# Hybrid transformer trunk on one core: the overflow loop three groups earlier, squares in the last group, second mixer's norm on VectorE

## The chip, the core and the metric

The kernel runs on one core of one Trainium2 chip. The metric is the device time of one execution in microseconds (us). A core has TensorE (PE; PEld are its weight loads), VectorE (DVE), ScalarE (ACT) and GpSimd (POOL), which work on tiles of 128 partitions in on-chip memory; matrix products are summed in eight PSUM banks. SyncE (SP) issues nearly all DMA transfers, in the order of its queue.

## What is computed

Two layers run over 256 latent and 256 context tokens of width 1024, in float32. Each layer is a mixer and a mixture of experts, each behind an RMS norm with shift and scale and added to the residual stream `h`. Layer 0's mixer is attention beside a gated delta net, layer 1's an RWKV-7. Cut to what matters:

```python
def rms_norm(x, gain):
    xf = x.astype(jnp.float32)
    y = xf * lax.rsqrt(jnp.mean(xf * xf, -1, keepdims=True) + EPS)
    return (y * gain.astype(jnp.float32)).astype(x.dtype)

def centred_shift(x):
    xp = jnp.pad(x, ((0, 0), (1, 1), (0, 0)))
    return 0.5 * (xp[:, :-2] + xp[:, 2:]) - x

# rwkv7_project: xx = centred_shift(x); xr, xw, xk, xv, xa, xg = [x + xx * mu[i] for i in range(6)]

# hier_moe: each token goes to 2 of the 32 experts of one layer; for a block of tokens xb of expert e
        hid = jax.nn.silu(xb @ w1[e]) * (xb @ w3[e])
        return out.at[toks].add((hid @ w2[e]) * ws[:, None]), None
```

An expert's `w1`, `w3` and `w2` are 2 MB each. All 32 experts of both layers are read in every execution.

## The kernel before

`h` is held as eight channel blocks of 128 x 512 (channels x tokens). `Trunk.run` calls the first mixer, `moe` for layer 0, the second mixer and `moe` for layer 1. A scheduler of the programming layer places the instructions of straight-line code on each engine's queue; it doesn't move them across a loop.

**The mixture.** `moe` serves the 32 experts in groups that share the 128 rows of a tile: two experts with up to 64 tokens each (a pair) or four with up to 32 (a quad). Layer 0 has 13 groups, here numbered 0 to 12: 8 and 12 are quads, 9 to 11 pairs. Layer 1 has 8 quads. Layer 0 orders its experts by load at run time (`sort`), so the loads of expert weights take their address from a register that SP reads from the table `order`. One group (`group`) does this: gather the group's tokens by one-hot products with the split tokens `ft` (two halves, each transposed), multiply by `w1` and `w3`, form the gated hidden rows, transpose them, multiply by `w2`, split the result in a high and a low part, and spread it back over the tokens with one product per channel block; `stt` on VectorE adds each to `h[k]` in two halves. `pipe(gens, 2)` keeps two groups in work, so that one group's gather stands between another's products. In the last group (`last`) the products with `w2` go expert by expert.

**Weights.** `weight` loads 1 MB at a time (`s<-in_moe_w` in the trace, line 173) into slots of the pool `big`, which has 21; `h` takes 2 of them and layer 0's `ft` 4. SP waits for a free slot and for the load eight before. Each group also takes one slot for its result `y`.

**Overflow jobs.** Tokens above an expert's share are left for jobs of up to 128 tokens. Their number `num` is only known at run time, so they are the body of a hardware loop, `tc.For_i(0, jobs, 1)` (line 794). All engines read the count and meet at the loop's start and end. With the inputs given no job is left, in either layer, and the body isn't run. `cut` says how many groups come ahead of the loop: all 13 in layer 0, 6 of 8 in layer 1. Where groups are left behind it, the loads of the next group's first weights (up to five) are issued ahead of it (`ahead`). `then` is `mixer1_weights`, which loads the second mixer's first weights.

**The norm.** `norm` squares the eight blocks on ACT (`squares`), adds them up in two sums on VectorE and GpSimd, sums over partitions with a product by ones, and takes logarithm and exponential for the inverse root. Each block is then multiplied (GpSimd in the second mixer) and scaled and shifted in two halves on ACT. The first mixer's norm, called with `between`, multiplies mostly on VectorE and then waits for the modulation. In the second mixer `each` follows per block: `xs` is the sum of the neighbours (VectorE or GpSimd), with its edges copied on GpSimd; two `stt` on VectorE give the shift `xx` and the operand `xk`, from which four matrix products per block start the keys.

Of the kernel before, what the change touches and what calls it, by code (L numbers as in the profile page):

```python
# [12 lines left out]
AF = mybir.ActivationFunctionType  # L13
OP = mybir.AluOpType
# [3 lines left out]
NTOK = 512  # L18
# [100 lines left out]
class Trunk:  # L119
# [169 lines left out]
                self.nc.vector.tensor_copy(h[k], ps)  # L289
        return h  # L290

    def squares(self, h, n):

        sums = [None, None]
        for k in range(8):
            sq = self.tmp()
            self.act(sq[:, :n], h[k], AF.Square)
            if k < 2:
                sums[k] = sq
            else:  # L300
                s = sums[k % 2]
                self.tt(s[:, :n], s[:, :n], sq[:, :n], OP.add, self.nc.vector if k % 2 else self.nc.gpsimd)
        return sums

    def norm(self, h, l, which, between=None, each=None):

        n = NTOK

        self.act(self.small([1, 1], "lnt"), self.eps[0:1, 5:6], AF.Ln)
        sums = self.squares(h, n)  # L310
        ps = self.bank()
        for i in range(2):
            self.mm(ps[:, :n], self.c["ones"], sums[i][:, :n], start=i == 0, stop=i == 1)
        rs = self.tmp()
        self.act(rs[:, :n], ps[:, :n], AF.Ln, bias=self.eps[:, 0:1], scale=1.0 / D)
        self.act(rs[:, :n], rs[:, :n], AF.Exp, scale=-0.5)
        u = self.chan(n)
        if between:
            for k in range(8):
                self.tt(u[k], h[k], rs, OP.mult, self.nc.gpsimd if k % 3 == 2 else None)  # L320
            between()
        for k in range(8):
            if not between:
                self.tt(u[k], h[k], rs, OP.mult, self.nc.gpsimd)
            for s in range(2):
                a = self.amul[:, l, which, k, s:s + 1]
                b = self.mcol[l][:, 3 * which, k, s:s + 1]
                x = u[k][:, 256 * s:256 * s + 256]
                if s and between:
                    self.ts(x, x, a, b, OP.mult, OP.add)  # L330
                else:
                    self.act(x, x, AF.Identity, scale=a, bias=b)
            if each:
                each(k, u[k])
        return u
# [299 lines left out]
        self.mm(out, r(onehot), r(hi), start, False)  # L635
        self.mm(out, r(onehot), r(lo), False, stop)

    def moe(self, l, h, lo, ahead, tokens, then=None):
        nc, c, I, tc = self.nc, self.c, self.I, self.tc
        n = NTOK - lo  # L640
        nt = n // 128
        logits, split = tokens
        sid, w, cnt, last, chosen = self.router(logits, nt)
# [4 lines left out]
        if l == 0:  # L648
            pairs = [((p, p + 1), (64, 64)) for p in range(5, 19, 2)]
            quads = [((p, p + 1, p + 2, p + 3), (32,) * 4) for p in range(19, 31, 4)]  # L650
            specs = [((0, 1), (64, 64)), ((2, 3), (64, 64)), ((4, 31), (96, 32)), pairs[0], quads[0]] + pairs[1:4]
# [2 lines left out]
            specs = [((p, p + 1, p + 2, p + 3), (32,) * 4) for p in range(0, 32, 4)]  # L654
        fixed = 4 if l == 0 else 32

        cut = (len(specs), 6)[l]
        table = order = sp = wp = None
        t4 = lambda: self.tmp(nt * 128).rearrange("p (t s) -> p t s", t=nt)
        half = lambda i: slice(512 * i, 512 * i + 512)  # L660
# [1 line left out]
        def group(P, wt, load, caps, last=False):  # L662
# [65 lines left out]
            for k in range(8):  # L728
                ps = self.bank()

                r = lambda a: a.bitcast(F32R)
                self.mm(ps[:, :n], r(y[:, 0, k, :]), r(PT), True, False)
                self.mm(ps[:, :n], r(y[:, 1, k, :]), r(PT), False, True)
                for s in range(lo // 256, 2):
                    ss = slice(256 * s - lo, 256 * s - lo + 256)
                    self.stt(h[k][:, ss], ps[:, ss], self.mcol[l][:, 5, k, s:s + 1], h[k][:, ss], OP.mult, OP.add)
                if k == 3:
                    yield

        def experts(spec, last):  # L740
            cols, caps = spec
            P = t4()
            step = cols[1] - cols[0]
            cs = slice(cols[0], cols[-1] + 1, step)
            places, weights = (sid, w) if cols[0] < fixed else (sp, wp)
            if len(set(caps)) == 1:
                G, cap = len(caps), caps[0]
                self.tt(P.rearrange("p t (g s) -> p t g s", g=G).bitcast(F32R),
                        c["iota"][:, None, None, :cap].to_broadcast([128, nt, G, cap]),
                        places[:, :, cs][:, :, :, None].to_broadcast([128, nt, G, cap]), OP.is_equal)  # L750
            else:
                a = 0
                for p, cap in zip(cols, caps):
                    self.tt(P[:, :, a:a + cap].bitcast(F32R), c["iota"][:, None, :cap].to_broadcast([128, nt, cap]),
                            places[:, :, p:p + 1].to_broadcast([128, nt, cap]), OP.is_equal)
                    a += cap
            yield
            regs = {}

            def load(name, g):  # L760
                p = cols[g]
                if p < fixed:
                    return ahead.pop((name, p), None) or self.weight(I[name][l, p])
                if p not in regs:
                    regs[p] = nc.sync.value_load(order[0:1, p:p + 1], min_val=0, max_val=31)
                return self.weight(I[name][l, bass.ds(regs[p], 1)].rearrange("o a b -> (o a) b"))

            yield from group(P, weights[:, :, cs], load, caps, last)

        def extra():  # L770
# [11 lines left out]
            sp, wp, order, rank = self.sort(nt, sid, cnt, chosen)  # L782
        table, num = self.overflow(nt, cnt, rank)
        drain(pipe(gens[:cut], 2))
        if cut >= len(specs):
            if then:
                then()
                then = None
        else:
            e0 = specs[cut][0][0]  # L790
            for name, g in [(m, g) for m in ("moe_w1", "moe_w3") for g in range(4)][:5]:
                ahead[name, e0 + g] = self.weight(I[name][l, e0 + g])
        jobs = nc.values_load(num, min_val=0, max_val=40, skip_runtime_bounds_check_because="counts bound it")
        with tc.For_i(0, jobs, 1):  # L794
            drain(extra())
# [638 lines left out]
    def mixer1(self, h):  # L1434
# [20 lines left out]
        def each(k, uk):  # L1455
            us = uk.rearrange("p (s t) -> p s t", s=2)
            xs = xx[k].rearrange("p (s t) -> p s t", s=2)
            self.tt(xs[:, :, 1:255], us[:, :, 0:254], us[:, :, 2:256], OP.add, nc.gpsimd if k % 2 else None)
            nc.gpsimd.tensor_copy(xs[:, :, 0:256:255], us[:, :, 1:255:253])
            self.stt(xx[k], xx[k], 0.5, uk, OP.mult, OP.subtract)  # L1460
            self.stt(xk[k], xx[k], mu[:, 2, k:k + 1], uk, OP.mult, OP.add)
            for m in range(4):
                self.mm(pk[m], wk0[k][:, 128 * m:128 * m + 128], xk[k], k == 0, k == 7)

        u = self.norm(h, 1, 0, each=each)
        pw, pa = self.bank(), self.bank()
        for i, w, ps in ((1, w1, pw), (4, a1, pa)):
            x = self.chan()
# [581 lines left out]
    def run(self):  # L2050
        h, u, fill = self.begin()
        ahead, tokens = self.mixer0(h, u, fill)
        self.mixer1_ahead()
        self.moe(0, h, 0, ahead, tokens, self.mixer1_weights)
        hl, ahead, tokens = self.mixer1(h)
        self.moe(1, hl, 256, ahead, tokens)
        self.store(hl)
# [26 lines left out]
```

## Time and profile before

| | |
|---|---|
| time, median of 3 runs | 2285.43 us |
| lowest of the 3 | 2277.39 us |
| profiled execution, its own time | 2273.31 us |
| its span, first to last instruction | 2271.5 us |
| TensorE busy, share of the span | 1899.7 us, 84% |
| VectorE, ScalarE, GpSimd busy | 834.1, 579.7, 367.0 us |
| mean granted TensorE clock | 0.885 of full |
| moved by DMA | 574.71 MB |

The trace is of one execution. A row of the timeline gives start, duration, engine, line, operation, output and input by the program's names, and the count of instructions merged in it; in brackets stands the idle time ahead of it and what ended that. A matrix product in float32 shows as two entries. Layer 0's mixture lies at about 615 to 1100 us, the second mixer to about 1780, layer 1's mixture to about 2265.

### The profile page before, as it was taken

What the parts mean: (1) busy time and instruction counts of PE and PEld (TensorE: products, weight loads), DVE (VectorE), ACT (ScalarE), POOL (GpSimd) and SP (SyncE); (2) the same over time, 40 slices, a digit from 0 to 9 for tenths busy, and PEclk for the clock granted to TensorE, in tenths of its full rate; (3) what the DMA queues carried; (4) which work ended last, traced back from release to release, by engine and by line L of the source; (5) the groups of instructions that cost most, each with busy time, mean ns of one, the idle gap of its engine ahead of it and who ended that gap; (6) DMA issues with size and microseconds to landing.
All of it is one profiled execution on the core that took longest, in us unless ns stands there. A gap on an engine that the chain in (4) does not pass through costs nothing.

```text
span 2271.5 us, 32246 instructions
## 1 busy us (share of the span) xinstructions
PE 1899.7 (84%) x12738; PEld 1066.3 (47%) x12738; DVE 834.1 (37%) x1885; ACT 579.7 (26%) x1200; POOL 367.0 (16%) x606
## 2 busy tenths in 40 slices
PE   5996899899899888998599599889897876666577
PEld 2443576567443344443245467757786522222222
DVE  3357335542432223132544955563823311111101
ACT  3363223330111111111324524534423100000000
POOL 1034154310000000000503731432501000000000
PEclk7998899999799999999799787787889788788789
DMA  9631132760099999999253543371865399999995
GB/s 312 221 130 38 43 113 100 264 249 22 1 387 421 421 421 421 421 421 417 90 186 101 171 151 140 113 258 59 302 209 221 138 422 421 422 421 421 386 422 247
DMA packets 161227, 574.71 MB, mean 253 GB/s; under 512 B 26218, under 2 KB 61073, under 8 KB 108593
## 3 DMA queue, kind: packets, MB, share of 16 engines
q1 hardware_dynamic: 158704, 572.36, 65.1%
q8 instruction: 102, 1.67, 0.3%
q10 hardware_dynamic: 2369, 0.25, 0.1%
q14 instruction: 52, 0.43, 0.1%
HBM read 537.66 MB, written 34.90 MB: 252 GB/s over the span
## 4 chain that ended last, share of the span: by engine, by line
PE 22%; DMA 18%; DVE 6%; issue 2%; ACT 2%; POOL 2%; SPq 0%; ACTq 0%; DVEq 0%; POOLq 0%
PE b L202 21%; DMA s<-in_moe_w 17%; DVE s L184 2%; DVE kb L184 1%; DVE s L193 1%; ACT t L197 1%; POOL s L184 1%; ACT s L197 1%; DVE t L184 1%; POOL t L184 1%; PE b L206 0%; DMA s<-vD 0%; DMA s<-kD 0%; DVE s L1940 0%; DVE t L1725 0%
## 5 line engine op out<-in xcount | busy, mean ns | idle before, releaser
L202 PE MATMUL b<-s 64*64 64x64 f32 (+7 forms) x5840 | 727.1, 300 | 59.0 <-DVE s L193 30.8
L202 PEld LDWEIGHTS b<-s 128*64 128x64 f32 (+4 forms) x5840 | 489.2, 163 | 294.7 <-issue 167.8
L202 PE MATMUL b<-s,kb 128*32 128x512 f32 (+1 forms) x2112 | 367.3, 654 | 81.1 <-DMA s<-in_moe_w 81.1
L202 PE MATMUL b<-s,t 128*32 128x512 f32 (+4 forms) x1544 | 349.6, 563 | 50.8 <-DMA s<-in_moe_w 24.9
L197 ACT ACTIVATE t<-b 128x512 f32<-128x512 f32 (+3 forms) x161 | 91.8, 573 | 729.8 <-PE b L202 446.3
L202 PEld LDWEIGHTS b<-s,t 128*32 128x32 f32 (+2 forms) x1544 | 156.4, 147 | 209.2 <-issue 125.9
L202 PEld LDWEIGHTS b<-s,kb 128*32 128x32 f32 (+1 forms) x2112 | 97.6, 126 | 327.2 <-issue 209.6
L197 ACT ACTIVATE s<-b 64x256 f32<-64x256 f32 (+6 forms) x228 | 114.4, 505 | 434.4 <-PE b L202 393.8
L202 PE MATMUL b<-t,s 128*128 128x512 f32 (+3 forms) x592 | 156.9, 411 | 16.7 <-ACT s L197 8.9
L184 DVE TENSOR_TENSOR s<-b,s 128x512 fp32r<-128x512 f32 (+3 forms) x90 | 52.8, 606 | 272.1 <-ACT s L197 264.5
L193 DVE SCALAR_TENSOR_TENSOR s<-b,mcol,s 128x256 f32<-128x256 f32 x296 | 120.9, 478 | 80.4 <-PE b L202 80.2
L206 PE MATMUL b<-cst,t 128*128 128x128 f32 (+1 forms) x466 | 79.5, 301 | 75.3 <-DVE t L193 35.3
L202 PEld LDWEIGHTS b<-t,s 128*128 128x128 f32 (+2 forms) x592 | 97.4, 197 | 74.9 <-ACT s L197 26.3
L206 PEld LDWEIGHTS b<-cst,t 128*128 128x128 f32 (+1 forms) x466 | 56.9, 161 | 121.6 <-issue 43.3
L193 DVE SCALAR_TENSOR_TENSOR t<-t,wc,b 128x512 f32<-128x512 f32 x21 | 15.7, 747 | 201.0 <-PE b L202 201.0
L1448 POOL MEMSET s<- 64x1024 f32 x2 | 1.9, 946 | 533.1 <-DVEq L794 533.1
L193 DVE SCALAR_TENSOR_TENSOR t<-t,b 128x512 f32<-128x512 f32 x21 | 14.5, 689 | 172.6 <-ACT t L197 172.6
L197 ACT ACTIVATE kb<-b 128x512 f32<-128x512 f32 (+2 forms) x92 | 50.1, 546 | 105.9 <-PE b L202 72.5
L202 PE MATMUL b<-t,cst 128*128 128x512 f32 (+6 forms) x64 | 36.6, 689 | 40.4 <-POOL t L184 19.3
L206 PE MATMUL b<-cst,s 128*128 128x128 f32 (+1 forms) x332 | 55.5, 303 | 17.3 <-DMA s<-in_ctx 8.2
L202 PE MATMUL b<-s,cs 128*32 128x512 f32 x384 | 53.8, 653 | 6.9 <-DMA s<-in_ada_w 6.3
L184 POOL TENSOR_TENSOR kb<-s 128x23 f32<-128x23 f32 (+11 forms) x115 | 46.4, 404 | 74.8 <-DVE s L1059 67.0
(241 smaller groups left out, 1676.6 us busy)
## 6 DMA issues: line engine op xcount, KB each, us to landing
s<-in_moe_w SPq DMA_DIRECT2D x384, 1024.0 KB, 19.8
s<-in_ada_w SPq DMA_DIRECT2D x48, 1024.0 KB, 8.7
s<-in_hy_w_in SPq DMA_DIRECT2D x8, 1024.0 KB, 5.0
sD<-s SPq DMA_DIRECT2D x8, 1024.0 KB, 4.5
s<-zD SPq DMA_DIRECT2D x8, 1024.0 KB, 5.5
s<-sD SPq DMA_DIRECT2D x8, 1024.0 KB, 8.1
s<-in_hy_w_out SPq DMA_DIRECT2D x4, 1024.0 KB
s<-in_rk_wk SPq DMA_DIRECT2D x4, 1024.0 KB, 9.0
```

The lines of the kernel that those rows point to most:

```text
L184: (eng or self.nc.vector).tensor_tensor(out=out, in0=a, in1=b, op=op)
L193: self.nc.vector.scalar_tensor_tensor(out, a, s, b, op0=op0, op1=op1)
L197: self.nc.scalar.activation(out, a, func, bias=bias, scale=scale)
L202: self.nc.tensor.matmul(out, lhsT, rhs, start=start, stop=stop, skip_group_check=skip)
L206: self.nc.tensor.transpose(out, a, self.c["ident"][:n, :n])
L1448: nc.gpsimd.memset(twa[64 * d:64 * d + 64].rearrange("p (i d t) -> p i d t", i=2, d=2)[:, :, 1 - d], 0.0)
```

## The change

`cut` is 10 in layer 0: the loop stands between groups 9 and 10, and the loads of group 10's `w1` and `w3` are issued ahead of it through `fetch`; registers are read again behind it. `then` is called after the last group. That group calls `tail(k)` after each updated block: `squares` now squares one block, adds it to its neighbour's on VectorE and sums each pair over partitions, so the product by ones is made four times. `norm` takes those sums as `ps`. In the second mixer the multiplication, the neighbour sums (VectorE) and the edge copies (ACT) leave GpSimd.

```diff
-    def squares(self, h, n):
...
+    def squares(self, ps, sums, h, k):
+
+        sq = self.tmp()[:, :NTOK]
+        self.act(sq, h[k], AF.Square)
+        sums.append(sq)
+        if k % 2:
+            self.tt(sums[k - 1], sums[k - 1], sq, OP.add)
+            self.mm(ps, self.c["ones"], sums[k - 1], k == 1, k == 7)
+
+    def norm(self, h, l, which, between=None, each=None, ps=None):
...
-        sums = self.squares(h, n)
-        ps = self.bank()
-        for i in range(2):
-            self.mm(ps[:, :n], self.c["ones"], sums[i][:, :n], start=i == 0, stop=i == 1)
+        if ps is None:
+            ps, sums = self.bank(), []
+            for k in range(8):
+                self.squares(ps, sums, h, k)
...
             if not between:
-                self.tt(u[k], h[k], rs, OP.mult, self.nc.gpsimd)
+                self.tt(u[k], h[k], rs, OP.mult)
...
-        cut = (len(specs), 6)[l]
+        cut = (10, 6)[l]
...
+                if last and tail:
+                    tail(k)
                 if k == 3:
                     yield
+
+        regs = {}
+
+        def fetch(name, p):
+            if p < fixed:
+                return self.weight(I[name][l, p])
+            if p not in regs:
+                regs[p] = nc.sync.value_load(order[0:1, p:p + 1], min_val=0, max_val=31)
+            return self.weight(I[name][l, bass.ds(regs[p], 1)].rearrange("o a b -> (o a) b"))
...
         drain(pipe(gens[:cut], 2))
-        if cut >= len(specs):
-            if then:
-                then()
-                then = None
-        else:
-            e0 = specs[cut][0][0]
-            for name, g in [(m, g) for m in ("moe_w1", "moe_w3") for g in range(4)][:5]:
-                ahead[name, e0 + g] = self.weight(I[name][l, e0 + g])
+        cols = specs[cut][0]
+        for name, p in [(m, p) for m in ("moe_w1", "moe_w3") for p in cols][:5]:
+            ahead[name, p] = fetch(name, p)
+        regs.clear()
         jobs = nc.values_load(num, min_val=0, max_val=40, skip_runtime_bounds_check_because="counts bound it")
...
-            self.tt(xs[:, :, 1:255], us[:, :, 0:254], us[:, :, 2:256], OP.add, nc.gpsimd if k % 2 else None)
-            nc.gpsimd.tensor_copy(xs[:, :, 0:256:255], us[:, :, 1:255:253])
+            self.tt(xs[:, :, 1:255], us[:, :, 0:254], us[:, :, 2:256], OP.add)
+            self.act(xs[:, :, 0:256:255], us[:, :, 1:255:253])
...
-        u = self.norm(h, 1, 0, each=each)
+        u = self.norm(h, 1, 0, each=each, ps=self.sums)
...
+        self.sums, sq = None, []
+
+        def tail(k):
+            if k == 0:
+                self.sums = self.bank()
+            self.squares(self.sums, sq, h, k)
+
-        self.moe(0, h, 0, ahead, tokens, self.mixer1_weights)
+        self.moe(0, h, 0, ahead, tokens, self.mixer1_weights, tail)
```

What this does to TensorE's queue in layer 0 is seen behind group 9's products with `w2`. `t` is the one-hot tile or hidden rows, `s` a slot (weights, tokens or `y`), `kb` the gathered tokens, `cst` the identity, `o_w` the weights of the tokens; in a gather the product reads `s,t` at 128x512, in the products with `w1` and `w3` it reads `s,kb` at 64x512, with `w2` `s,t` at 64x512, and in the output `t,s`. Before, from group 9's output to group 10's products with `w2`:

```order
L202 MATMUL b<-t,s 128x512 x4
L202 MATMUL b<-s,t 128x512 x8
L202 MATMUL b<-t,s 128x512 x4
L206 MATMUL b<-cst,t 128x128 x4
L202 MATMUL b<-s,t 128x512 x8
L206 MATMUL b<-cst,t 128x128 x8
L202 MATMUL b<-o_w,t 128x2 x4
L202 MATMUL b<-t,s 128x512 x8
L202 MATMUL b<-s,kb_5923 64x512 x32
```

After, from the loop's end on (the loop's body is left out), to group 11's output:

```order
L788 UNCONDITIONAL_BRANCH
L202 MATMUL b<-s,t 128x512 x8
L206 MATMUL b<-cst,t 128x128 x4
L202 MATMUL b<-s,t 128x512 x8
L206 MATMUL b<-cst,t 128x128 x8
L202 MATMUL b<-o_w,t 128x2 x4
L202 MATMUL b<-s,kb_6173 64x512 x16
```

```order
L202 MATMUL b<-s,kb_6173 64x512 x16
L202 MATMUL b<-s,kb_6245 64x512 x16
L206 MATMUL b<-cst,t 128x128 x4
L202 MATMUL b<-s,kb_6245 64x512 x16
L202 MATMUL b<-s,t 64x512 x10
L206 MATMUL b<-cst,t 128x128 x4
L202 MATMUL b<-s,t 64x512 x6
L202 MATMUL b<-t,s 128x512 x8
L202 MATMUL b<-s,t 64x512 x2
L202 MATMUL b<-t,s 128x512 x8
L202 MATMUL b<-s,t 64x512 x14
L202 MATMUL b<-t,s 128x512 x16
```

Group 9's output of 16 now stands whole ahead of the loop, and group 10's gather starts behind it; between the two blocks shown stands group 11's gather, of the same five rows. Groups 10 and 11 then run side by side, and group 12's gather follows group 11's output.

On VectorE, at the end of layer 0, `s<-b,mcol` are the updates of `h`, `t<-t` the sums of squares, `s<-s,t` the norm's product, `s<-s 128x2x254` the neighbour sums. Before, from the last updates through the loop (its body left out) to the second mixer's first operand:

```order
L184 TENSOR_TENSOR s<-b,s 128x8x64 x2
L193 SCALAR_TENSOR_TENSOR s<-b,mcol_97,s 128x256 x16
L793 TENSOR_LOAD j_num
L794 COMPARE_AND_BRANCH
...
L569 MEMSET j_tab 128x32
L582 MEMSET j_tab 128x32
L184 TENSOR_TENSOR t<-t 128x512 x3
L184 TENSOR_TENSOR s<-s 128x2x254 x2
L193 SCALAR_TENSOR_TENSOR s<-s 128x512
L193 SCALAR_TENSOR_TENSOR s<-s,mu 128x512
```

After, over the same work:

```order
L184 TENSOR_TENSOR s<-b,s 128x8x64 x2
L193 SCALAR_TENSOR_TENSOR s<-b,mcol_97,s 128x256 x4
L184 TENSOR_TENSOR t<-t 128x512
L193 SCALAR_TENSOR_TENSOR s<-b,mcol_97,s 128x256 x6
L184 TENSOR_TENSOR t<-t 128x512
L193 SCALAR_TENSOR_TENSOR s<-b,mcol_97,s 128x256 x6
L184 TENSOR_TENSOR t<-t 128x512 x2
L184 TENSOR_TENSOR s<-s,t 128x512 x4
L184 TENSOR_TENSOR s<-s 128x2x254 x4
L193 SCALAR_TENSOR_TENSOR s<-s 128x512 x4
L193 SCALAR_TENSOR_TENSOR s<-s,mu 128x512
```

The loop is gone from this place, the sums of squares stand between the updates, and norm and shift go in fours of blocks on VectorE alone.

## Rows read from the trace of the kernel before

**Rows 1.** The page: span, and the expert loads (count, size, us to landing).

```profile
span 2271.5 us, 32246 instructions
...
s<-in_moe_w SPq DMA_DIRECT2D x384, 1024.0 KB, 19.8
```

**Rows 2.** Windows: start:end, length, busy us (count) of each engine, clock, DMA share, GB/s.

```profile
core 0: us, PE busy (x) PEld busy (x) DVE busy (x) ACT busy (x) POOL busy (x), PEclk, DMA share, GB/s
905.00:1047.00 142.00, 126.82 (x633) 62.02 (x631) 37.17 (x86) 20.61 (x36) 0.00 (x0) 0.98 1.01 421
```

**Rows 3.** Waits of TensorE, 905 to 1095: us in total, times, longest.

```profile
PE b L202 <- DMA s<-in_moe_w: 6.6, 3, 3.8
```

**Rows 4.** Timeline of TensorE, groups 9 to 12 of layer 0.

```profile
948.81 7.08 PE L202 MATMUL b<-s,kb 128*64 128x512 f32 x30 [0.55 <-DMA s<-in_moe_w]
...
966.51 1.20 PE L202 MATMUL b<-t,s 128*128 128x512 f32 x4 [0.69 <-ACT s L197]
...
992.70 2.11 PE L202 MATMUL b<-s,t 128*128 128x512 f32 x8
...
1000.58 7.14 PE L202 MATMUL b<-s,t 128*64 128x512 f32 x32
...
1048.04 7.92 PE L202 MATMUL b<-s,kb 128*32 128x512 f32 x70
...
1058.29 7.05 PE L202 MATMUL b<-s,kb 128*32 128x512 f32 x58 [2.32 <-DMA s<-in_moe_w]
...
1067.68 22.59 PE L202 MATMUL b<-s,t 128*32 128x512 f32 x64 [0.69 <-ACT t L197]
```

**Rows 5.** Windows around the loop of layer 1.

```profile
2144.00:2148.00 4.00, 0.00 (x0) 0.00 (x0) 0.00 (x0) 0.00 (x0) 0.00 (x0) 0.50 0.54 225
2148.00:2152.00 4.00, 2.04 (x4) 1.17 (x4) 0.76 (x2) 0.00 (x0) 0.00 (x0) 0.50 0.45 119
2152.00:2160.00 8.00, 6.62 (x23) 4.20 (x22) 0.62 (x4) 2.67 (x5) 0.00 (x0) 0.50 1.02 426
```

**Rows 6.** Timeline behind the loop of layer 1.

```profile
2149.48 0.76 DVE L184 TENSOR_TENSOR t<-cst,r_sid 128x256 fp32r<-128x256 f32 x2 [16.07 <-DMA s<-in_moe_w]
2149.96 2.08 PE L202 MATMUL b<-s,t 128*128 128x512 f32 x4 [18.88 <-DVE t L184]
2158.35 1.92 PE L202 MATMUL b<-s,kb 128*32 128x512 f32 x4
```

**Rows 7.** Timeline from layer 0's last output into the second mixer.

```profile
1090.96 4.00 PE L202 MATMUL b<-t,s 128*128 128x512 f32 x16 [0.69 <-ACT s L197]
1093.13 6.36 DVE L193 SCALAR_TENSOR_TENSOR s<-b,mcol,s 128x256 f32<-128x256 f32 x16 [1.50 <-PE b L202]
1099.87 4.28 ACT L197 ACTIVATE t<-s 128x512 f32<-128x512 f32 x8 [8.96 <-DVEq L794]
...
1106.59 3.78 PE L202 MATMUL b<-t,cst 128*128 128x512 f32 x4 [11.63 <-POOL t L184]
...
1110.41 0.69 ACT L197 ACTIVATE t<-b,eps 128x512 f32<-128x512 f32 x1 [4.96 <-PE b L202]
...
1112.41 0.63 ACT L197 ACTIVATE t<-t 128x512 f32<-128x512 f32 x1
...
1122.27 5.62 PE L202 MATMUL b<-s 128*128 128x512 f32 x8 [11.90 <-DVE s L193]
...
1125.05 1.10 ACT L197 ACTIVATE s<-s,mcol,amul 128x256 f32<-128x256 f32 x2 [0.58 <-POOL s L184]
...
1126.08 1.75 DVE L193 SCALAR_TENSOR_TENSOR s<-s 128x512 f32<-128x512 f32 x1
...
1129.56 22.58 PE L202 MATMUL b<-s 128*128 128x512 f32 x52 [1.67 <-DVE s L193]
...
1143.12 0.68 DVE L193 SCALAR_TENSOR_TENSOR s<-s 128x512 f32<-128x512 f32 x1
```

**Rows 8.** Loads of weights, 2090 to 2200: shortest, median, longest way to landing.

```profile
DMA to landing us min/median/max: 5.3/19.8/20.1
```

More of the change, by code (lines that the diff above doesn't have):

```diff
@@ L290, in load_h @@
         return h
-    def squares(self, h, n):
[L294 to L299, printed above, removed]
-            else:
[L301 to L305, printed above, removed]
+    def squares(self, ps, sums, h, k):
[6 more added lines that the diff above has]
+    def norm(self, h, l, which, between=None, each=None, ps=None):
         n = NTOK
         self.act(self.small([1, 1], "lnt"), self.eps[0:1, 5:6], AF.Ln)
-        sums = self.squares(h, n)
-        ps = self.bank()
-        for i in range(2):
-            self.mm(ps[:, :n], self.c["ones"], sums[i][:, :n], start=i == 0, stop=i == 1)
+        if ps is None:
+            ps, sums = self.bank(), []
+            for k in range(8):
+                self.squares(ps, sums, h, k)
         rs = self.tmp()
@@ L636, in pick, with moe @@
         self.mm(out, r(onehot), r(lo), False, stop)
-    def moe(self, l, h, lo, ahead, tokens, then=None):
+    def moe(self, l, h, lo, ahead, tokens, then=None, tail=None):
         nc, c, I, tc = self.nc, self.c, self.I, self.tc
@@ L757, in experts @@
             yield
[L758 to L766, printed above, removed]
+            load = lambda name, g: ahead.pop((name, cols[g]), None) or fetch(name, cols[g])
             yield from group(P, weights[:, :, cs], load, caps, last)
@@ L784, in moe @@
         drain(pipe(gens[:cut], 2))
-        if cut >= len(specs):
-            if then:
-                then()
-                then = None
-        else:
-            e0 = specs[cut][0][0]
-            for name, g in [(m, g) for m in ("moe_w1", "moe_w3") for g in range(4)][:5]:
-                ahead[name, e0 + g] = self.weight(I[name][l, e0 + g])
+        cols = specs[cut][0]
+        for name, p in [(m, p) for m in ("moe_w1", "moe_w3") for p in cols][:5]:
+            ahead[name, p] = fetch(name, p)
+        regs.clear()
         jobs = nc.values_load(num, min_val=0, max_val=40, skip_runtime_bounds_check_because="counts bound it")
```

## The prediction, made before the changed kernel was run

> **What bounds the kernel now.** I read the page first, then the weight stream's stretch, then both loops, then the gap between layer 0's mixture and layer 1's mixer. The profiled span is 2271.5 us; expert weights arrive as 384 loads of 1 MB [rows 1]. Between 905 and 1047 us, in the later half of layer 0's mixture, DMA moves 421 GB/s, so one load takes 1.0486 MB / 421 GB/s = 2.49 us, and TensorE is busy for 126.8 of 142 us [rows 2]. So two resources stand near their limit, and the question is which has room. From 905 to 1095 us TensorE waited for weights only 6.6 us in all, three times [rows 3]. The last two of them are in the timeline: 0.55 us at 948.8 and 2.32 us at 1058.3 [rows 4]. Between those two, TensorE took every weight later than it landed: there it, and not DMA, sets the pace, with 2.3 us to spare at the end of the stretch. A hole cut into TensorE there comes out at the end except for 2.3 us.
>
> The loop in layer 1 shows what an overflow loop in mid-stream does, with no jobs to run (nothing of its body executes). TensorE's idle time before it was 18.88 us, and VectorE's 16.07 us ended on a weight load: the loop starts only when every load issued ahead of it has landed [rows 6]. DMA falls to 225 and 119 GB/s for two stretches of 4 us, against 421: (1 - 344/842) x 8 = 4.7 us of stream lost. The granted clock is 0.50 there and still 0.50 to 2160 us [rows 5].
>
> **The loop in layer 0 moved to after group 9.** I count groups 0 to 12. When does the drain end? At 948.8 the third load of group 9's w3 landed; until the last of group 10's w3 come 1 + 4 (w2) + 4 + 4 = 13 loads, x 2.49 = 32.4, so 981.2. SP's order up to there is that of before. In layer 1 the stream's equivalent end is 2144 + 4 x 225/421 = 2146.1 and TensorE restarts at 2149.96, 3.8 later [rows 5, 6]; VectorE's comparison ahead of it is twice as wide in layer 0, +0.3. Restart: 985.3. Without a next group to interleave, TensorE ends group 9's output at 966.5 + 4.0 = 970.5 [rows 4, 7], and VectorE's 6.4 us behind it are over by 977: both wait for DMA. TensorE stands 14.8 us.
>
> The gather that follows takes 1000.58 - 992.70 = 7.9 us at full clock [rows 4]. In layer 1 after the loop it took 2158.35 - 2149.96 = 8.4 at half clock, and there it has 4 matmuls where layer 0 has 8, twice, 2.08 per 4 [rows 6]: 8.4 + 4.2 = 12.6. So w1 of group 10 starts at 997.9. From there to w1 of group 12 TensorE does, in the order shown, six passes of 7.14 over a pair's weights, two gathers of 7.9, two outputs of 4.0 with 0.7 of waiting ahead of each [rows 4, 7]: 42.8 + 15.8 + 9.4 = 68.0, so 1065.9. Before it was 1048.0: 17.9 late. The 2.3 us wait for w3 disappears, as those weights land earlier than TensorE now asks. Group 12's w2 starts 15.6 us late, and its 22.6 us and all behind are unchanged. **+15.6.**
>
> Is DMA covered? Of 21 slots h holds 2 and the split tokens 4; group 10's prefetch holds 8, so 7 loads go out at once, 17 us of stream, by which time TensorE frees the first of group 10. Later frees stay ahead of the 24 loads of group 12, whose last slots come when its own w1 is half read. I take no cost; the bounds of the whole term are 4.7 (the lost stream alone) and 15.6 + 2.3 + 7 (the wait stays and the first pass runs at half clock too) = 25. The two added register loads on SP stand ahead of the stream, with the other 28, where SP waits for slots.
>
> **Squares in the last group.** Before: from the first update (1093.13) through the loop, 8 squares on ACT (4.28), adds on GpSimd and VectorE, the sum over partitions (3.78 for four entries at half clock), logarithm and exponential to 1113.04 is 19.9 us [rows 7]. After, VectorE does the 16 updates (6.4) with four adds of 0.68 between them and about 0.5 waiting for the first square: 9.6. Then one pair's ones matmul, 1.9, with 0 to 1.2 queued from the pair before, and the same 2.6 to the end of the exponential: 14.1 to 15.3. **-5.2** in the middle. ACT's squares (0.54 each) hide behind the updates, the table load behind the adds. If the clock has not yet fallen, it is -7; if the adds hold up the updates, -4.6.
>
> **Norm and shift on VectorE.** The instructions leave GpSimd: 8 products, 4 shifted sums, 8 edge copies (to ACT). Beside GpSimd a scalar_tensor_tensor took 1.75, alone 0.68 [rows 7]. VectorE thus spends 4 x 0.68 = 2.7 us per channel, not 4.0. But what counts is TensorE, which runs without a break from 1129.56, 16.5 after the exponential, for far longer than this stage. The new order takes channels in fours: four ACT channels of 1.1 end 5.2 after the exponential, then the edges, the last sum, four updates and the first operand: 9.3, as before (1122.27 is 9.2). Its 8 entries last 5.6 [rows 7], to 14.9; the second to fourth operand are there by 13.9, the next four by 22, TensorE needing 3.5 per channel. So the unbroken run starts 1.6 sooner. **-1.5**; bounds 0 and -4 (full clock from the start).
>
> Costed at nothing: the first mixer's norm, now with four ones matmuls and all adds on VectorE. It waits afterwards for modulation weights; without that cover it would cost 1.9. Layer 1's loop and its prefetch keep their place, and the downstream order differs in small exchanges only.
>
> **Sum:** 15.6 - 5.2 - 1.5 = +8.9 on the profiled execution's 2273.3 (its span and 1.8 around it): 2282.2. That execution was faster than both shown figures, the lowest run 2277.4 and the median 2285.4. I place the sum on 2277.4: **2286.3 us**.
>
> **The rivals.** *DMA sets the pace after all.* If TensorE's passes can be packed closer, only the 4.7 of lost stream stay: 4.7 - 5.2 - 1.5 = -2.0, so 2275.4 (2271.3 on the profiled execution). For it: 421 GB/s without a dent. Against it: no wait for weights between 948.8 and 1058.3. The Trainium skill, "Perfetto Trace Analysis", section Identifying the Most-Contended Engine, calls matmul busy time a poor measure and wants LDWEIGHTS busy time instead; that is 62.0 of 142 us here, 44%, which would leave TensorE room and speaks for this rival. The waits in the trace speak against that reading. *The end gains more.* If the last sum meets no queue and all of GpSimd's interference was on the path, 7 + 4 are gained and with the stream alone lost the sum is -6.3: 2271.1. *TensorE restarts worse:* the 25 us bound with the small gains, 25 - 4.6 = +20: 2297.8. *Weights starve after the loop.* If slots come free too late, each of the seven weight passes not prefetched waits for a landing, at least 5.3 us [rows 8]: 8.9 + 37 = +46, 2323. It decides once fewer than about 7 loads go out at the restart; the slot count speaks against it. *The change does not do what it says* would be a loop waiting with nothing prefetched: the same starvation, in part.
>
> **How the numbers follow.** A difference of 2% is 46 us, about what a measurement of this kernel can tell from no change. Chances: forecast 0.70 (2277 to 2294 with the runs' own spread), DMA sets the pace 0.14, end gains more 0.05, worse restart 0.08, starvation 0.02, and 0.01 for something over 2% faster that I do not see. The range takes in the first four: 2270 to 2300. Faster 0.01, same 0.97, slower 0.02.
>
> **What would show it.** In the changed profile: the new loop near 970 to 985 us, TensorE idle about 15 us, granted clock 0.50 behind it; DMA below 421 GB/s for about 8 us; TensorE's w1 of group 12 near 1066 with no wait for weights on w3; exponential 14 to 15 us after the first update of group 12; scalar_tensor_tensor at 0.68 in the norm; unbroken matmuls some 15 us after the exponential, about 9 us later in the span than 1129.6. I am wrong if TensorE waits for weights after the loop, or if group 12 starts less than 8 us late.

## The result, and the profile after

The changed kernel takes **2293.17 us** in the median of five runs (2288.76 to 2297.52), beside 2280.81 for the kernel before. The ratio is 1.0058, 95% interval 1.003 to 1.0085: 7 to 19 us longer, clear of no change but under the 2% that the prediction calls a difference. One of the five executions of the kernel before took 5072.04 us, more than twice the others; without it their median is 2279.1, and the difference 14.1 us in place of 12.4. The prediction was 2286.3 us in a range of 2270 to 2300, so 6.9 too low.

The profiled execution took 2296.36 us, its page:

```profile
span 2294.6 us, 32277 instructions
...
PE 1919.8 (84%) x12746; PEld 1080.8 (47%) x12746; DVE 831.6 (36%) x1899; ACT 579.6 (25%) x1208; POOL 334.6 (15%) x580
```

GpSimd lost 32 us of work and TensorE gained 20, with nearly the same instructions: its mean granted clock was 0.881, before 0.885.

**The loop after group 9.** TensorE's timeline, and under it the row of before that [rows 4] lacks, group 9's products with `w2`:

```profile
942.36 7.08 PE L202 MATMUL b<-s,kb 128*64 128x512 f32 x30 [0.40 <-DMA s<-in_moe_w]
...
951.71 7.65 PE L202 MATMUL b<-s,t 128*64 128x512 f32 x32 [0.69 <-ACT t L197]
...
960.05 4.00 PE L202 MATMUL b<-t,s 128*128 128x512 f32 x16 [0.69 <-ACT s L197]
...
976.53 3.78 PE L202 MATMUL b<-s,t 128*128 128x512 f32 x8 [12.47 <-DVE t L184]
...
987.98 7.09 PE L202 MATMUL b<-s,kb 128*64 128x512 f32 x32
...
1059.95 13.94 PE L202 MATMUL b<-s,kb 128*32 128x512 f32 x128
...
1076.20 22.59 PE L202 MATMUL b<-s,t 128*32 128x512 f32 x64 [0.69 <-ACT t L197]
```

```profile
958.17 7.65 PE L202 MATMUL b<-s,t 128*64 128x512 f32 x32 [0.69 <-ACT t L197]
```

TensorE stands 12.5 us ahead of group 10's gather, which then takes 11.5 us (976.53 to 987.98), mostly at half clock (1.2 GHz; the granted clock is 0.50 to 982 us). `w1` and `w3` of group 12 run through without a wait. From group 9's first product with `w2` to group 12's it is 1076.20 - 951.71 = 124.5 us; before, 1067.68 - 958.17 = 109.5 [rows 4]. That is **+15.0 us**. VectorE names the cause of the standstill, and windows show the stream and the clock:

```profile
975.78 0.69 DVE L184 TENSOR_TENSOR t<-cst,o_sid 128x512 fp32r<-128x512 f32 x1 [7.19 <-DMA s<-in_moe_w]
```

```profile
core 0: us, PE busy (x) PEld busy (x) DVE busy (x) ACT busy (x) POOL busy (x), PEclk, DMA share, GB/s
968.00:972.00 4.00, 0.00 (x0) 0.00 (x0) 0.59 (x2) 0.00 (x0) 0.00 (x0) 0.53 0.89 369
972.00:976.00 4.00, 0.00 (x0) 0.00 (x0) 0.22 (x1) 0.00 (x0) 0.00 (x0) 0.50 0.22 90
976.00:980.00 4.00, 3.47 (x8) 2.48 (x8) 1.13 (x4) 0.00 (x0) 0.00 (x0) 0.50 0.83 281
...
1004.00:1008.00 4.00, 4.00 (x20) 1.29 (x18) 0.00 (x0) 0.00 (x0) 0.00 (x0) 1.00 0.35 94
```

The stream loses 5.0 us around the loop and falls off once more at 1004, where SP waits 10.3 us for a product of TensorE before it can load again. TensorE does not notice: from 955 to 1110 us none of its waits is for weights.

**The end of layer 0.** TensorE, then ACT, then VectorE; [rows 7] is the same stretch before:

```profile
1099.48 1.46 PE L202 MATMUL b<-t,s 128*128 128x512 f32 x4 [0.69 <-ACT s L197]
1103.94 1.22 PE L202 MATMUL b<-t,cst 128*128 128x512 f32 x2 [3.00 <-DVE t L184]
1104.47 4.92 PE L202 MATMUL b<-t,s 128*128 128x512 f32 x12
...
1112.24 1.98 PE L202 MATMUL b<-t,cst 128*128 128x512 f32 x4 [1.83 <-DVE t L184]
1126.92 44.00 PE L202 MATMUL b<-s 128*128 128x512 f32 x96 [12.70 <-issue]
```

```profile
1114.31 1.28 ACT L197 ACT_TABLE_LOAD   x1 [2.06 <-PE b L202]
1115.60 0.69 ACT L197 ACTIVATE t<-b,eps 128x512 f32<-128x512 f32 x1
...
1117.60 0.63 ACT L197 ACTIVATE t<-t 128x512 f32<-128x512 f32 x1
```

```profile
1100.75 1.66 DVE L193 SCALAR_TENSOR_TENSOR s<-b,mcol,s 128x256 f32<-128x256 f32 x4 [0.59 <-PE b L202]
1103.10 0.69 DVE L184 TENSOR_TENSOR t<-t 128x512 f32<-128x512 f32 x1 [0.69 <-ACT t L197]
1106.05 2.58 DVE L193 SCALAR_TENSOR_TENSOR s<-b,mcol,s 128x256 f32<-128x256 f32 x6 [2.26 <-PE b L202]
...
1123.67 2.49 DVE L193 SCALAR_TENSOR_TENSOR s<-s 128x512 f32<-128x512 f32 x4
```

After four of its 16 entries the output stops: the first pair's product by ones (`t,cst`) stands next in TensorE's queue, waits 3.0 us for squares and sum, and the other 12 entries of the output wait behind it, so VectorE's updates stop 2.26 us too. From the start of the output to the end of the exponential it is 1118.23 - 1099.48 = 18.75 us, before 1113.04 - 1090.96 = 22.08 [rows 7].

To follow a gain into the second mixer I take as its mark a short product (output 2 x 36, `t,cst`) behind the keys. From the start of group 12's output it comes 78.5 us later before (1169.41) and 73.0 after (1172.45): **-5.5 us** for the whole end.

Up to this mark the profiled execution after is only 3.0 us behind that of before, and at the end of the span 23.1. Two things follow: it was ahead when it came to group 9, and it lost some 20 us in the second mixer (617.9 us against 597.4). Both are taken up below.

### The profile page after: what moved, and what is told of

Read it like the earlier page. It is cut to its first block, busy times and chain, and to the rows that moved or that the text cites. A ratio compares the mean times of both kernels' runs of the same rounds, so it can differ in the third digit from the quotient of the medians.

```text
span 2294.6 us, 32277 instructions
## 1 busy us (share of the span) xinstructions
PE 1919.8 (84%) x12746; PEld 1080.8 (47%) x12746; DVE 831.6 (36%) x1899; ACT 579.6 (25%) x1208; POOL 334.6 (15%) x580
## 4 chain that ended last, share of the span: by engine, by line
PE 54%; DMA 26%; DVE 9%; issue 5%; ACT 4%; POOL 2%; SPq 0%; ACTq 0%; DVEq 0%; POOLq 0%
PE b L202 50%; DMA s<-in_moe_w 23%; PE b L206 4%; DVE s L184 3%; ACT t L197 2%; DVE kb L184 1%; DVE t L193 1%; DVE t L184 1%; ACT s L197 1%; POOL s L184 1%; DVE s L193 1%; DMA s<-in_ada_w 1%; DMA sD<-s 0%; DMA ab<-in_ada_b 0%; ACT L197 0%
## 5 line engine op out<-in xcount | busy, mean ns | idle before, releaser
L202 PE MATMUL b<-s 64*64 64x64 f32 (+7 forms) x5840 | 737.9, 305 | 57.2 <-ACT s L197 18.6
L202 PEld LDWEIGHTS b<-s 64*64 64x64 f32 (+4 forms) x5840 | 498.7, 167 | 294.9 <-issue 183.1
L202 PE MATMUL b<-s,kb 128*32 128x512 f32 (+1 forms) x2112 | 361.2, 644 | 80.1 <-DMA s<-in_moe_w 80.1
L202 PE MATMUL b<-s,t 128*32 128x512 f32 (+4 forms) x1544 | 358.0, 577 | 62.6 <-DVE t L184 29.6
L202 PE MATMUL b<-t,s 128*128 128x512 f32 (+3 forms) x592 | 162.1, 423 | 19.0 <-ACT s L197 9.6
L206 PE MATMUL b<-cst,s 128*128 128x128 f32 (+1 forms) x332 | 56.3, 306 | 19.9 <-DVE s L184 10.5
L202 PE MATMUL b<-t,cst 128*128 128x512 f32 (+6 forms) x72 | 38.0, 644 | 31.3 <-ACT t L197 10.7
L206 PEld LDWEIGHTS b<-cst,s 128*128 128x128 f32 (+1 forms) x332 | 43.2, 159 | 33.7 <-issue 22.5
L197 ACT ACTIVATE s<-s 64x128 f32<-64x128 f32 (+2 forms) x122 | 38.9, 320 | 75.0 <-DVE s L184 73.1
```

The lines of the kernel that those rows point to most:

```text
L197: self.nc.scalar.activation(out, a, func, bias=bias, scale=scale)
L202: self.nc.tensor.matmul(out, lhsT, rhs, start=start, stop=stop, skip_group_check=skip)
L206: self.nc.tensor.transpose(out, a, self.c["ident"][:n, :n])
```

## The experiments

Each is set against the kernel before, timed beside it on the same chip. Marks in the profiles give each stage apart from the spread of the others (us): *mixture*, from group 9's `w2` to group 12's; *end*, from group 12's output to the 2 x 36 product; *mixer*, from there to layer 1's first router product. From that to the end it is 504 to 505 in all of them. The kernel before, profiled twice more, has a mixture of 109.4 and 111.1, the changed kernel once more 124.4.

| kernel | mixture | end | mixer | median less before's | ratio, interval |
|---|---|---|---|---|---|
| before (profile) | 109.5 | 78.5 | 597.4 | | |
| changed | 124.5 | 73.0 | 617.9 | +12.4 | 1.0058, 1.003 to 1.0085 |
| loop alone | 124.6 | 74.5 | 606.5 | +20.5 | 1.0099, 1.0066 to 1.0132 |
| no loop | 109.8 | 72.7 | 596.7 | -7.5 | 0.997, 0.9943 to 0.9998 |
| no tail, loop at the end | 109.5 | 72.1 | 613.6 | +1.2 | 1.0013, 0.9991 to 1.0035 |
| norm and shift alone | 109.5 | 76.0 | 607.5 | +1.3 | 1.0003, 0.9979 to 1.0027 |
| break, no loop | 109.7 | 73.9 | 606.9 | one run, -9.5 | |
| late products by ones | 124.6 | 73.4 | 602.5 | one run, -1.6 | |
| only `w1` ahead | 117.4 | 73.0 | 610.3 | +2.0 | 1.0017, 0.9995 to 1.0038 |

**The loop alone.** The kernel before with these parts of the change: `cut`, `fetch`, the prefetch, `then` at the end.

```diff
-        cut = (len(specs), 6)[l]
+        cut = (10, 6)[l]
```

> The kernel before with the loop of layer 0 moved to after group 9, its prefetch with it; squares, norm and shift as before. My theory (TensorE sets the pace in the later half of layer 0's mixture, so its standstill is handed through): from group 9's w2 to group 12's w2 about 15 us more than before's 109.5, and the median about 15 us above before, with the end of layer 0 as before. Rival, DMA sets the pace: 4.7 us more. Rival, the time is lost in the second mixer: less than 10 us between the two w2, and over 5 us between the second mixer's values (1169.7 before) and the last of it.

The mixture takes 15.1 us more, as TensorE's pace says, and not 4.7. The median is 20.5 longer where I expected 15, and the end is 4.0 *shorter* where I expected no change: the two stages make 11.1, and where the other 9 us lie is not shown. The end is shorter with the old squares because, with no loop between, ACT starts them behind the first update and not behind the last.

```profile
1111.56 6.36 DVE L193 SCALAR_TENSOR_TENSOR s<-b,mcol,s 128x256 f32<-128x256 f32 x16 [1.51 <-PE b L202]
...
1112.53 1.35 ACT L197 ACTIVATE t<-s 128x512 f32<-128x512 f32 x2 [3.20 <-DVE s L193]
...
1126.84 0.63 ACT L197 ACTIVATE t<-t 128x512 f32<-128x512 f32 x1
```

That is 0.97 us after the updates begin; before it was 1099.87 - 1093.13 = 6.74 [rows 7]. The exponential ends 1127.47 - 1109.38 = 18.1 us after the start of the output (before 22.1), and so sooner than the changed kernel's 18.75.

**No loop in layer 0.** This drops overflow jobs, of which there are none here.

```diff
+        if l == 0:
+            drain(pipe(gens, 2))
+            then()
+            return
         drain(pipe(gens[:cut], 2))
```

> The changed kernel with layer 0's loop over overflow jobs left out altogether (the data of this case has no such jobs; any there would be dropped): groups 10 to 12 follow group 9 without a break, squares go with the last group, norm and shift on VectorE. My theory: the time from group 9's w2 to group 12's w2 is before's 109.5 again, the end gains 2 to 5 us behind group 12's output, and the whole is 5 to 9 us under before and 15 to 17 us under the changed kernel. Rival, the second mixer loses time from its own new order: it stays within 3 us of before.

The mixture is that of before, the end 5.8 us shorter, and the whole 7.5 us under before with an interval just clear of none. So the change without any loop in layer 0 gains, and the loop in its new place takes all of that and more: against the changed kernel it is 20 us, where I expected 15 to 17.

**A break without a loop.** Groups 10 to 12 start anew, the prefetch stays, only the loop is missing (it drops overflow jobs too).

```diff
         regs.clear()
+        if l == 0:
+            drain(pipe(gens[cut:], 2))
+            then()
+            return
         jobs = nc.values_load(num, min_val=0, max_val=40, skip_runtime_bounds_check_because="counts bound it")
```

> The changed kernel with the break after group 9 and the prefetch of group 10 kept, but no loop in layer 0 (overflow jobs, of which this data has none, would be dropped). My theory: the 12.5 us standstill comes from the loop's wait for all loads in flight, so TensorE restarts 1 to 3 us behind group 9's output at full clock; from group 9's w2 to group 12's w2 110 to 114 us (before 109.5, changed 124.5). Rival, the lost interleaving of groups is what costs: 118 us or more.

The mixture takes 109.7 us. TensorE's timeline shows the gather on the heels of the output, at a granted clock of 1.00:

```profile
962.76 4.00 PE L202 MATMUL b<-t,s 128*128 128x512 f32 x16 [0.69 <-ACT s L197]
966.60 2.03 PE L202 MATMUL b<-s,t 128*128 128x512 f32 x8
```

TensorE has no wait for weights from 955 to 1110 us here, where before has the 2.3 us at 1058. So the break with its prefetch costs 0.2 us net, within the spread of before (109.4 to 111.1), and the other 14.8 of the 15 us are the loop's own.

**Only `w1` ahead of the loop.** Four loads instead of eight.

```diff
-        for name, p in [(m, p) for m in ("moe_w1", "moe_w3") for p in cols][:5]:
+        for name, p in [(m, p) for m in ("moe_w1", "moe_w3") for p in cols][:5 if l else 2]:
```

> The changed kernel, but in layer 0 only w1 of group 10 is fetched ahead of the loop (4 loads in place of 8). My theory, the standstill is the wait for the last load in flight: 4 loads less end it up to 10 us sooner, so VectorE's updates end it, as with the loop after group 7 (6.9 us in place of 12.5), and the gather finds less of the low clock (9.5 us in place of 11.5); w3 lands in time. From group 9's w2 to group 12's w2 116 to 119 us in place of 124.5, the median 5 to 8 us under the changed kernel. Rival, the prefetch is needed: TensorE waits for w3 behind the loop, 122 us or more, no gain.

```profile
961.35 4.00 PE L202 MATMUL b<-t,s 128*128 128x512 f32 x16 [0.69 <-ACT s L197]
971.94 3.78 PE L202 MATMUL b<-s,t 128*128 128x512 f32 x8 [6.60 <-DVE t L184]
...
981.43 7.09 PE L202 MATMUL b<-s,kb 128*64 128x512 f32 x32
```

```profile
971.20 0.69 DVE L184 TENSOR_TENSOR t<-cst,o_sid 128x512 fp32r<-128x512 f32 x1 [1.32 <-issue]
```

```profile
963.00:971.00 8.00, 2.34 (x11) 1.54 (x9) 6.36 (x16) 0.00 (x0) 0.00 (x0) 0.91 0.13 53
```

The standstill is 6.6 us. VectorE's updates end at 969.9 and its next operation waits for no load any more; the gather takes 9.5. The mixture is 7.1 shorter than in the changed kernel, 117.4. The stream lost more than there: 7.0 us in the window shown (8 x (1 - 53/421)), and TensorE still waited for no weight up to 1110 us. That speaks against DMA as the pace of this stretch. It is the best version with the loop at this place, level with before and not under it.

**The loop at other places.** `cut` 4 and 8, each ahead of a quad, with four matrices fetched ahead (eight loads, as in the changed kernel).

```diff
-        cut = (10, 6)[l]
+        cut = (4, 6)[l]        # the other kernel: (8, 6)
-        for name, p in [(m, p) for m in ("moe_w1", "moe_w3") for p in cols][:5]:
+        for name, p in [(m, p) for m in ("moe_w1", "moe_w3") for p in cols][:4 + l]:
```

> The changed kernel with the loop after group 3 (ahead of the first group of four experts), four matrices of the next group fetched ahead. My theory, TensorE late by 17.3 us behind the loop and the stream by 4.7: the waits for weights that before has from there on (2.65, 1.61, 0.44, 3.75, 0.55, 2.32, in all 11.3) vanish and take that much of it, so group 12's w2 starts 6 us later than without a loop (4.7 to 9), and the median is 6 to 10 us under the changed kernel. Rival, a loop costs the same wherever it stands: 15 us as in the changed kernel, the same median.

> The same with the loop after group 7, ahead of the second group of four. My theory: of the waits, 3.75, 0.55 and 2.32 are still to come, 6.6 in all, so group 12's w2 starts 17.3 - 6.6 = 10.7 us later than without a loop (9 to 13). Rival, the same cost wherever it stands: 15 us. Rival, the stream sets the pace: 4.7.

My account fell here. Measured from group 0's last transposes of gathered tokens to group 12's `w2` (466.9 us before, 482.9 changed) it is 492.2 with the loop after group 3 and 481.9 after group 7: 25.3 and 15.0 longer, where I expected 6 and 10.7. Of these, 3.5 and 2.2 lie ahead of the loop, up to the start of the output of group 3 and of group 7 (139.7 and 288.0 us, before 136.2 and 285.8), so 21.8 and 12.8 are behind it. The median of the former is 2308.16 us, ratio 1.0122 (1.0089 to 1.0155); the latter ran once, in 2296.56 us.

The standstill itself is shorter, 6.9 us in both. As many loads stand ahead of the loop as in the changed kernel, but the stream is further ahead of TensorE here: it has all but stopped 3 us into the 4 us output of group 7 (a row of windows below), and in the changed kernel only 13 us after the start of group 9's. So VectorE's updates end the standstill, and not a load. Behind it the groups run in another phase, with both of a couple gathered before either's `w2`, and for the loop after group 3 the stream stops a second time. First a window of the loop after group 7, then two windows and the waits of TensorE of the loop after group 3:

```profile
889.00:893.00 4.00, 0.61 (x3) 0.17 (x1) 4.00 (x12) 0.00 (x0) 0.00 (x0) 1.00 0.04 16
```

```profile
730.00:745.00 15.00, 7.38 (x32) 4.26 (x29) 8.84 (x22) 1.19 (x2) 0.00 (x0) 0.84 0.40 145
910.00:925.00 15.00, 13.07 (x95) 6.39 (x96) 1.35 (x6) 3.23 (x6) 0.00 (x0) 1.00 0.52 198
```

```profile
PE b L206 <- ACT t L197: 13.5, 18, 1.2
PE b L202 <- DMA s<-in_moe_w: 7.6, 4, 3.1
```

The two windows lose 9.8 and 7.9 us of stream, of the waits for weights 7.6 us are left of 11.3, and those for ACT rise from 9.5 to 13.5. With the loop after group 7, group 8's `w1` starts 9.6 us late, counted from group 7's output (906.02 - 885.61 against 897.26 - 886.49), and not 17.3; but of the 6.6 us of waits that I let vanish, 4.6 are there (1.56 and 3.06). That its 12.8 us lie in the expected 9 to 13 is luck, and what makes them up is not broken down further.

**Products by ones behind all outputs.** Meant to take the stop out of TensorE's queue.

```diff
-            self.mm(ps, self.c["ones"], sums[k - 1], k == 1, k == 7)
+        if k == 7:
+            for i in range(0, 8, 2):
+                self.mm(ps, self.c["ones"], sums[i], i == 0, i == 6)
```

> The changed kernel with the four products with ones behind the last pair's sum, none between the outputs of group 12. My theory: TensorE no longer stands 3.0 us ahead of the second part of group 12's output, and the exponential ends 15 to 16.5 us after the start of that output where the changed kernel took 18.75. Rival, the chain behind the last sum is what counts, four products at the end in place of one: 18 us or more.

```profile
1099.94 4.00 PE L202 MATMUL b<-t,s 128*128 128x512 f32 x16 [0.69 <-ACT s L197]
1109.22 6.65 PE L202 MATMUL b<-t,cst 128*128 128x512 f32 x8 [5.28 <-DVE t L184]
```

The stop is gone, but the sums then came behind all updates, and eight entries, at a granted clock of 0.55, took 6.65 us. The exponential ends 19.9 us after the output's start (1119.88), worse than 18.75. The rival was right.

**Norm and shift alone, and all but the tail.** In the kernel before the product, sums and edges leave GpSimd. In the other, the changed kernel, the loop goes back to the end of layer 0 and the squares, in their new form, behind it.

```diff
# norm and shift alone
-                self.tt(u[k], h[k], rs, OP.mult, self.nc.gpsimd)
+                self.tt(u[k], h[k], rs, OP.mult)
-            self.tt(xs[:, :, 1:255], us[:, :, 0:254], us[:, :, 2:256], OP.add, nc.gpsimd if k % 2 else None)
-            nc.gpsimd.tensor_copy(xs[:, :, 0:256:255], us[:, :, 1:255:253])
+            self.tt(xs[:, :, 1:255], us[:, :, 0:254], us[:, :, 2:256], OP.add)
+            self.act(xs[:, :, 0:256:255], us[:, :, 1:255:253])
# no tail: cut is len(specs) again, with before's branch for it, and
-        self.moe(0, h, 0, ahead, tokens, self.mixer1_weights, tail)
+        self.moe(0, h, 0, ahead, tokens, self.mixer1_weights)
-        u = self.norm(h, 1, 0, each=each, ps=self.sums)
+        u = self.norm(h, 1, 0, each=each)
```

> The kernel before with only the norm's product, the shift's sums and its edges taken from GpSimd (products and sums on VectorE, edges on ACT); squares, tail and loop as before. My theory: 1 to 2 us under before (bounds 0 and 4), from the exponential to the second mixer's unbroken matmuls. Rival, VectorE and ACT get in the way of what follows and the second mixer is longer: 2 to 10 us over before, its loss behind 1180 us.

> The changed kernel with the loop of layer 0 back at the end and all squares behind it, in the new form (sums of pairs on VectorE, four products with ones); norm and shift on VectorE. My theory: no hole in the mixture, the first mixer's norm some 3 us shorter as in the changed kernel, the second's between nothing and 4 us shorter: 3 to 6 us under before, about 15 under the changed kernel. Rival, the second mixer loses time with norm and shift on VectorE: not under before.

Norm and shift alone bring 2.4 us at the end, all but the tail 6.4. That is 0.9 more than the changed kernel gets with the tail. The timeline of ACT and TensorE without a tail:

```profile
1089.49 3.99 PE L202 MATMUL b<-t,s 128*128 128x512 f32 x16 [0.69 <-ACT s L197]
...
1098.39 4.27 ACT L197 ACTIVATE t<-s 128x512 f32<-128x512 f32 x8 [8.95 <-DVEq L793]
...
1100.47 5.08 PE L202 MATMUL b<-t,cst 128*128 128x512 f32 x8 [7.00 <-DVE t L184]
...
1102.68 1.28 ACT L197 ACT_TABLE_LOAD   x1
...
1107.59 0.63 ACT L197 ACTIVATE t<-t 128x512 f32<-128x512 f32 x1
```

Here the exponential ends 1108.22 - 1089.49 = 18.73 us after the output's start, against 18.75 with the tail. The products by ones run beside the squares, and the first table load hides behind them. In neither kernel did the local gain reach the median, which stays within 1.3 us of before, where I expected 1 to 2 and 3 to 6 under it. In their profiles the mixer is longer (607.5 and 613.6 us), which is next to the spread of one program below; that norm and shift on VectorE cause it is not shown.

**The second mixer once more.** Two more executions of before (2281.00 and 2278.84 us) and one of the changed kernel (2287.44 us).

> The kernel before once more, for the second mixer: from its values to layer 1's first router product the profiled executions took 597.4 us before and 617.9 changed. Theory, this is the granted clock's spread from execution to execution: further executions of both lie in 597 to 618 without order. Rival, the second mixer's own order in the changed program costs 10 us or more: this one at 603 or under.

> The changed kernel once more, for the same stretch. Theory, spread: it may come as low as 600. Rival, its own order: 612 or over.

> The kernel before a third time, for the same stretch: spread, anywhere in 597 to 618; rival, 603 or under again.

Windows of the mixer as marked, first before in the execution of [rows 1], then before again twice, then the changed kernel in its two:

```profile
1169.41:1766.84 597.43, 529.37 (x5382) 394.89 (x5383) 310.83 (x672) 247.47 (x486) 184.20 (x307) 0.83 0.50 168
```

```profile
1168.09:1774.56 606.47, 535.68 (x5383) 396.18 (x5383) 311.13 (x672) 246.85 (x486) 183.39 (x307) 0.82 0.49 165
```

```profile
1173.45:1772.27 598.82, 530.72 (x5383) 396.16 (x5383) 310.02 (x672) 246.87 (x486) 183.88 (x307) 0.83 0.49 167
```

```profile
1172.45:1790.31 617.86, 548.07 (x5383) 408.69 (x5383) 313.00 (x672) 246.53 (x485) 182.11 (x307) 0.80 0.48 161
```

```profile
1174.03:1781.09 607.06, 536.12 (x5382) 398.14 (x5383) 313.56 (x672) 246.51 (x485) 182.45 (x307) 0.82 0.49 164
```

The instructions are the same, the other engines' work hardly differs, and TensorE's busy time grows as the granted clock falls from 0.83 to 0.80. Its idle time is 68 to 71 us in all five (mixer less busy), and 68 to 73 in all fourteen profiles: what differs is time in which TensorE works, and not what it waits for. One program spreads by 9 to 11 us here, so spread alone is large; before's second execution (606.5) is above the 603 that the rival wanted and its third (598.8) under it, and the changed kernel's second is under its 612. But their means are 600.9 and 612.5, so a difference of the programs beside it isn't excluded. It stays open.

## Why the prediction was right or wrong

**What bounds the mixture:** right. TensorE's pace carried the standstill to the end, with the loop alone and in the changed kernel alike, and the stream had room. The rival that DMA sets the pace is out here, by the kernel with only `w1` ahead above all. The measure set beside it, weight-load busy time of the Trainium skill, "Perfetto Trace Analysis", section Identifying the Most-Contended Engine, does not fit this stretch: weight loads are busy for 55.6 of 142 us after, 39%, and TensorE paces it nevertheless (the section names the share of peak arithmetic beside it, which was not worked out here). The window of [rows 2], after:

```profile
905.00:1047.00 142.00, 121.10 (x570) 55.56 (x562) 31.72 (x73) 17.01 (x29) 0.00 (x0) 0.93 0.96 393
```

**The loop:** 15.6 predicted, 15.0 measured, with its parts close: standstill 14.8 from the end of the output's work, measured 12.5; half-clock gather 12.6, measured 11.5; from there to group 12's `w1` 68.0, measured 72.0: the two passes over `w2`, each in pieces between the other group's work, took 9.0 us and not 7.14. The wait of 2.3 vanished as said, and 1.0 more with it: group 12's `w1` and `w3` run through in 13.94 us, before in 7.92 and 7.05. So the parts are off by -2.3, -1.1, +4.0 and -1.0, and the close total is in part luck. The mechanism holds: I had counted with loads landing to the last one issued ahead, and that is what VectorE's row shows.

**The tail:** the step that failed in size and in reason. I put -5.2 on squares among the updates, with the updates held up for about 0.5 us. TensorE's in-order queue held them for 2.26, and the table load, costed at nothing, stood on the path behind the last product (1.28). From the first update to the end of the exponential it went from 19.9 to 17.5, so -2.4; from the output's start -3.3. And that gain is not the tail's: with the old squares the loop leaving this place gives 4.0 at the end and an exponential after 18.1 us, and new squares behind a loop at the end give the same 18.7. With norm and shift's 2.4 beside the 4.0 the end would be 6.4 shorter without the tail, an estimate, where the changed kernel's is 5.5 shorter. What the tail needs, a loop that stands earlier, cost 15.

**Norm and shift:** -1.5 predicted, -2.4 measured alone, -2.2 in the changed kernel (exponential to the 2 x 36 product: 56.4 before, 54.2 after). `scalar_tensor_tensor` fell from 1.75 to 0.62 as foreseen. My sign for it, unbroken products 15 us after the exponential, did not show the gain: they start 8.7 after, and run at half clock at first (granted clock 0.50 to 1130 us).

The end in all, -6.7 predicted, -5.5 measured: near by the luck of two errors.

**Costed at nothing, the first mixer's norm:** wrong. Its sums on VectorE start TensorE's products by ones sooner, and these end at 24.2 us in place of 25.9. Before and after at the start of the span:

```profile
22.16 3.78 PE L202 MATMUL b<-t,cst 128*128 128x512 f32 x4 [7.71 <-POOL t L184]
...
49.05 8.70 PE L202 MATMUL b<-s 128*128 128x432 f32 x16 [1.24 <-ACT s L197]
```

```profile
18.36 5.85 PE L202 MATMUL b<-t,cst 128*128 128x512 f32 x8 [4.41 <-DVE t L184]
...
47.11 7.51 PE L202 MATMUL b<-s 128*128 128x432 f32 x16 [1.24 <-ACT s L197]
```

The last products that wait for modulation weights start sooner too (41.8 us, before 42.9), so the cover that I named moved along. Group 0's last transposes in layer 0 start at 599.4 to 603.9 us in five executions with the old squares (mean 602.1) and at 593.3 to 599.3 in nine with the new (mean 595.3): -6.8 us, of which the rows above show 1.9; the rest is not broken down. So the unbroken products of the second mixer, which I put some 9 us later in the span than 1129.6, start at 1126.9.

**The sum.** Measured pieces: -6.8 to layer 0's mixture, +1.0 in its earlier groups, +15.0, -5.5: +3.7. The medians differ by 12.4. Of the stages measured, only the second mixer can hold the missing 9 us, and that fits the means of its five executions (+11.6); but with a spread of 10 in each program its size isn't established, and why it would be longer (a chance of order, or of the time at which it starts) is not shown. The 6.9 by which 2293.17 exceeds 2286.3 are 3.4 of the base, 2277.4 where the median is 2280.81, and 3.5 of the sum, 8.9 where it is 12.4. That the sum came so near is luck beside the loop's term: two terms that I put at nothing, -5.8 ahead of group 9 and some +9 in the second mixer, cancel in large part.

## What to carry to other kernels

The hardware loops here, in mid-stream, waited for every load issued ahead of them, even with no pass to run: price such a loop as the drain of these loads, or the work of the other engines where that ends later, plus the low clock behind it, and issue ahead only what is needed before the next load lands. Before work is put among another engine's in-order stream, see what stands behind it in that queue. Gains of a few us found at one place can go under in a stage whose clock spreads by more, so measure each stage by its own marks.

## What the runs showed of the hardware

The second mixer of one program varied with TensorE's granted clock (0.80 to 0.83) between 597.4 and 606.5 us before and between 607.1 and 617.9 us after, with TensorE's idle time alike within 3 us and the other engines' busy times within 4 us. Taking half of the prefetch away made the kernel shorter: standstill 6.6 in place of 12.5 us, mixture 7.1 less, though the stream stopped for longer.
